# An expert stage with its overflow loop first, stores on another queue, aligned tiles, and a second norm moved into the gather

## The chip, the cores and the metric

The kernel runs on one core of one Trainium2 chip. The metric is the device time of one launch in microseconds, as the median of several runs. The engines are named as in the profile: PE is TensorE's matmul and PEld its weight load, DVE is VectorE, ACT is ScalarE, POOL is GpSimd, and SP is SyncE, which only issues transfers here. Each of SP, ACT and POOL can issue transfers on a queue of its own; a "q" behind an engine's name is its sequencer.

## The reference, cut to what matters

512 tokens of 1024 float32 values go through two transformer blocks. In the first, two mixers run side by side (a gated linear recurrence and a sparse attention), their outputs are merged and multiplied by `w_out`, and a layer norm follows. Then come a second norm with a scale and shift made from a conditioning vector, a router over 32 experts in 4 groups, two experts for each token, and a further layer norm. The second block is a causal attention and a gated feed-forward network, both with modulated RMS norms. The part that the change touches:

```python
mod = c_act @ ada_w[l] + ada_b[l]
sh1, sc1, g1, sh2, sc2, g2 = jnp.split(mod, 6, axis=-1)
...
y = (1 + g1[:, None]) * (merged @ w_out[l])
x = _layer_norm(ALPHA * x + y) * ln1_g[l] + ln1_b[l]
h = _layer_norm(x) * (1 + sc2[:, None]) + sh2[:, None]
y = (1 + g2[:, None]) * _hier_moe(h, router_grp_w[l], router_grp_b[l], ...)
x = _layer_norm(ALPHA * x + y) * ln2_g[l] + ln2_b[l]
...
return (jax.nn.silu(xb @ w1[e]) * (xb @ w3[e])) @ w2[e]      # one expert, 1024 -> 512 -> 1024
```

An expert has 6 MB of weights (three float32 matrices of 2 MB), so the 32 experts have 192 MB, and each of them is read once.

## The kernel before, in words

**Stages.** The first stage (up to about 735 us) computes the two mixers. Its large products go through `mm3` (lines 93 to 95): each operand is split into a high and a low part, and three matmuls (high by high, low by high, high by low) are added up in PSUM. Lines 75 and 77 split the weights as they arrive, ScalarE the high part and VectorE the low one. `finish_t1` (lines 1439 to 1533) does the product with `w_out`, the layer norm, the second norm and the router's logits; `router` ranks the tokens. `t2` (lines 487 to 769) is the expert stage. The rest, from about 1360 us, is the second block, with `mm3` again.

**The way from the output product to the first expert.** `finish_t1` multiplies in four blocks of 128 tokens by four column blocks of 256. After a block's last column, `layer_norm` (lines 166 to 185) makes the block's `x1`. Two things follow for each block: `logits` (lines 258 to 270) transposes x1 and multiplies it by the router's weights, whose scale has been folded in; `norm` (lines 272 to 277) makes the second norm, with two VectorE passes over 128x1024 (lines 181 and 183) that read their columns in a permuted order, a ScalarE copy to the high part `h2hi`, and a GpSimd subtraction for the low part. `SC2` and `SH2` are the scale and shift spread over all 128 partitions. A table `order` (lines 517 to 519) says which of these steps stand behind which product. The router then works on small tiles, mostly on VectorE, and gives each of the 1024 token copies a row: rows 64e to 64e + 63 belong to expert e, and rows from 2048 on hold what doesn't fit into 64.

**Tokens and experts.** `gather` (lines 500 to 529) builds a one-hot matrix from the rows and multiplies it by the high and low parts of the second norm (line 525, 64 matmuls for four experts), so that the tokens of four experts come out transposed, 64 columns each; lines 527 and 528 evict half of them by ScalarE and half by VectorE. `up` (line 541) multiplies the 64 tokens by w1 and w3, 16 matmuls each, and evicts (line 548). `act` transposes, applies the gate function (Silu, line 557, ScalarE) and multiplies (line 558, VectorE). `down` (line 570) multiplies by w2; line 575 applies g2 into a tile `y` (three buffers), and line 603 stores `y` to a DRAM array `yscr` with a DMA on GpSimd's queue. In program order expert e + 1's `up` stands ahead of expert e's `down`.

**Weights.** `Stream` (lines 410 to 456) holds a ring of 15 places of 1 MB for the expert weights: 4 tiles of its own, 3 `raw` tiles that the first stage's weights use too, 4 "late" tiles, which are there when the first stage has ended, and 4 pairs of `whi` and `wlo` parts. Each load (1 MB, line 454, or two halves, line 450) is issued by SP when its place has come free. The program issues 16 loads ahead of the experts (lines 468 to 484), the others as the ring goes round.

**The overflow loop.** `general` (lines 676 to 700) is a loop on the device over blocks of 64 tokens for experts with more than 64. With the timed inputs it makes no trip. It stands ahead of expert 18 (`CUT`, line 718); expert 18's `up` isn't issued ahead of expert 17's `down` then, and lines 737 to 742 issue the loads for the next places ahead of the loop. Line 679 is the loop's head, where all engines meet; line 720 is expert 18's `up` behind it.

**Behind the experts.** `late` (lines 648 to 674) reloads x1 and fetches the rows of `yscr`, and lines 753 to 766 add them up and apply the last layer norm.

**Order of the work.** The program is written in one order, and a planner with a cost model moves instructions of an engine within what the data allow; `issue_after` fixes a place. SBUF tiles come from pools, in which a tile stands wherever the one before it ended.

Of the kernel before, what the change touches and what calls it, by code (L numbers as in the profile page):

```python
# [9 lines left out]
F32 = mybir.dt.float32  # L10
F32R = mybir.dt.float32r
BF = mybir.dt.bfloat16
# [14 lines left out]
class G:  # L27
    pass

# [136 lines left out]
def layer_norm(g, pool, x, total, gain, bias, out, tag, accum=None, perm=False):  # L166
# [11 lines left out]
    if perm:  # L178
        x, gain, bias = (t.rearrange("q (p k) -> q k p", k=8) for t in (x, gain, bias))
        out = out.rearrange("q (k p) -> q k p", k=8)  # L180
    nc.vector.scalar_tensor_tensor(out, x, mv[:, 0:1], gain, op0=ALU.add, op1=ALU.mult)
    nc.vector.reciprocal(mv[:, 1:2], mv[:, 1:2])
    g.last_norm = nc.vector.scalar_tensor_tensor(out, out, mv[:, 1:2], bias, op0=ALU.mult, op1=ALU.add,
# [4 lines left out]
def iota(g, pool, shape, pattern, name, chan=0):  # L188
    t = pool.tile(shape, F32, name=name)
    g.nc.gpsimd.iota(t, pattern=pattern, base=0, channel_multiplier=chan, allow_small_or_imprecise_dtypes=True)  # L190
    return t


def route_state(g, pool):
# [10 lines left out]
    r.iot = iota(g, pool, [128, 256], [[1, 256]], "iot")  # L205
    r.pidx = iota(g, pool, [128, 1], [[0, 1]], "pidx", 1)
    r.II = pool.tile([128, 64], F32, name="II")
    nc.vector.tensor_tensor(r.II, g.ident[:, 0:64], g.ident[:, 64:128], op=ALU.add)


class Front:
# [3 lines left out]
    def __init__(self, g, pool, work, pp, ptags, x1d, sc2, sh2, mods, w_rg, w_re, b_rg, b_re):  # L215
        nc = g.nc
        self.g, self.pool, self.work, self.pp, self.ptags, self.x1d = g, pool, work, pp, ptags, x1d
        self.sc2, self.sh2, self.mv = sc2, sh2, {}
# [7 lines left out]
        cols = pool.tile([128, 2, 8], F32, name="cols")  # L226
# [45 lines left out]
    def norm(self, i, x, total, h2):  # L272

        g = self.g
        self.mv[i] = layer_norm(g, self.work, x, total, self.sc2, self.sh2, h2, "h2", perm=True)
        g.nc.scalar.activation(g.h2hi[:, i], h2, AF.Copy)
        g.nc.gpsimd.tensor_tensor(g.x_tile(F32R)[:, 0], h2, g.h2hi[:, i].bitcast(F32), op=ALU.subtract)
# [8 lines left out]
def router(g, f, pp, ptag, pbufs):  # L286

    nc, r, rp = g.nc, g.route, f.pool
# [38 lines left out]
    for i in range(4):  # L327
        for j in range(i):
            nc.tensor.matmul(rps[:, i], f.oneb, M[:, j], start=(j == 0), stop=False)
        nc.tensor.matmul(rps[:, i], f.tri, M[:, i], start=(i == 0), stop=True)  # L330
    gt = rp.tile([128, 32, 7], F32, name="gt")
# [18 lines left out]
    def rest(pool):  # L350
# [29 lines left out]
        nc.vector.scalar_tensor_tensor(r.row, ro, dx, r.row, op0=ALU.mult, op1=ALU.add)  # L380
        nc.vector.tensor_copy(r.rowi, r.row)
# [12 lines left out]
        nc.vector.tensor_scalar(r.obase, ok, 64.0, 1984.0, op0=ALU.mult, op1=ALU.add)  # L394
# [12 lines left out]
CUT = 18  # L407
# [55 lines left out]
def t2_early(g, pool, w1, w3, w2):  # L463

    st = g.stream = Stream(g, w1, w3, w2)
    st.add(pool, 4)
    st.add("raw", g.ws.nraw)
    for e in range(2):
        for j, h in UP:
            st.fetch(e, j, h)  # L470


def t2_ahead(g):

    st = g.stream
    for n in (4,):
        st.add(g.es2.enter_context(g.tc.tile_pool(name="t2late%d" % n, bufs=1, side="right", reuse_waits="tile")), n)
    st.add("parts", g.ws.nhi)
    for h in range(2):
        st.fetch(0, 2, h)  # L480
    for j, h in UP:
        st.fetch(2, j, h)
    for h in range(2):
        st.fetch(1, 2, h)


def t2(g, yscr, x1d, g2, ln2g_, ln2b_, ahead):
# [5 lines left out]
    with es:  # L493
        pp = es.enter_context(tc.tile_pool(name="t2p", bufs=1, space=PSUM))
        ee = es.enter_context(ExitStack())
        eg = ee.enter_context(tc.tile_pool(name="t2g", bufs=1, side="right"))

        h2 = [g.h2hi[:, i] for i in range(4)], [t[:, 0] for t in g.xt[F32R]]

        def gather(nblk, base, between=None):  # L500
# [9 lines left out]
            for i in range(4):  # L510
                o1 = eg.tile([128, 256], F32, name="o1", tag="o1", bufs=2)[:, :n]
# [7 lines left out]
            def step(s):  # L519
                ps = pp.tile([128, 8, 64], F32, name="gps", tag="gps", bufs=2)  # L520
                for k in range(8 // nblk):
                    c = 128 * (8 // nblk * s + k)
                    for i in range(4):
                        for q, part in enumerate(h2):
                            nc.tensor.matmul(ps[:, k * nblk:k * nblk + nblk], part[i][:, c:c + 128], oh[:, i],  # L525
                                             start=(i + q == 0), stop=(i + q == 4))
                nc.scalar.copy(xg[:, 8 * s:8 * s + 4], ps[:, 0:4])
                nc.vector.tensor_copy(xg[:, 8 * s + 4:8 * s + 8], ps[:, 4:8])
# [22 lines left out]
        def act(t):  # L551
# [4 lines left out]
            sg = ep.tile([128, 4, 64], F32, name="sg", tag="sg", bufs=4)  # L556
# [4 lines left out]
        def down(sgs, raw, stores):  # L561
# [10 lines left out]
            for yp, store in zip(yps, stores):  # L572
                if callable(store):
                    y = ep.tile([128, 512], F32, name="y", tag="y", bufs=3)
# [23 lines left out]
        def store_at(row):  # L598
# [4 lines left out]
            return lambda y: nc.gpsimd.dma_start(yscr[row:row + 64].rearrange("r (h n) -> h r n", h=2), y)  # L603
# [25 lines left out]
        def onehot_last():  # L629
# [4 lines left out]
            for i in range(4):  # L634
                o1 = eg.tile([128, 256], F32, name="o1", tag="o1", bufs=2)[:, 0:128]
# [40 lines left out]
        def general(lraw):  # L676

            nrun = nc.values_load(r.nov[0:1, 0:1], min_val=0, max_val=NOV - 1)
            with tc.For_i(0, nrun, 1):
# [4 lines left out]
                one = indirect_weights(r.eb[:, 0:1], lraw)  # L684
# [21 lines left out]
        ep = ee.enter_context(tc.tile_pool(name="t2e", bufs=1))  # L706
# [8 lines left out]

        s_ = behind(0, up(sources(0), raw(0)))
        for e in range(32):
            if e == CUT:
                general(lraw)
                s_ = behind(e, up(sources(e), raw(e)))  # L720

            ts = up(sources(e + 1), raw(e + 1)) if e + 1 not in (CUT, 32) else None
# [12 lines left out]
            elif e + 1 == CUT:  # L735

                n, lraw = st.n, alloc()
                todo = [x for k in range(6) for x in [(CUT + k,) + u for u in UP] +
                        [(CUT + k - 1, 2, h) for h in range(2 if k else 0)]]
                for x in todo:  # L740
                    if st.n - n < len(st.ring):
                        st.fetch(*x)
# [8 lines left out]
        with tc.tile_pool(name="t2f", bufs=1) as fp:  # L751
# [160 lines left out]
def t1(g, d):  # L912
# [3 lines left out]
    with top:  # L916
# [3 lines left out]
        hp = eh.enter_context(tc.tile_pool(name="t1h", bufs=1))  # L920
# [925 lines left out]
```

## Time and profile before

| | before |
|---|---|
| median of 3 runs | 2033.7 us (2032.71 to 2036.41) |
| profiled execution, its own time | 2033.85 us |
| its span | 2032.1 us |
| TensorE's mean granted clock | 0.969 |
| PE busy | 1900.2 us (94%) |
| DVE busy | 1013.8 us (50%) |
| ACT busy | 637.3 us (31%) |
| POOL busy | 111.9 us (6%) |
| moved by DMA | 394.75 MB, mean 194 GB/s |

How to read it: the span is the time from the first to the last recorded instruction, and the profiled execution's own time is a little longer. A share of busy time is a mean over stages that have different limits: the experts' weights are read in the slices from 820 to 1340 us, where the page shows about 405 GB/s, against 30 to 300 in the other slices. A busy share of the DMA is a mean over the core's 16 DMA engines. A matmul's duration overlaps its neighbours', so the step from one start to the next is what it costs in a run of them. The chain of waits names, for each stretch of the span, what the last work was waiting for; "issue" is time without a wait that the profile shows.

### The profile page before, as it was taken

To read this page: it belongs to the slowest core of one execution; us is meant where nothing else is said; L and a number is where in the kernel's file an instruction comes from. 1 tells how busy PE (TensorE), PEld (TensorE's weight loads), DVE (VectorE), ACT (ScalarE), POOL (GpSimd) and SP (SyncE) were. 2 spreads that over 40 slices of the span, in tenths; PEclk is the share of its full clock that TensorE was granted. 3 is DMA by queue.
4 is the path that set the end of the run, shared out by engine and by line. 5 is a ranking of instruction groups with operands and counts; after the bars stand their busy time and mean duration, and the time that the engine had idled before them with its cause. 6 is when DMAs were issued, how large, how long until landed. Compare 5 with 4: busy or idle time off the path is not lost.

```text
span 2032.1 us, 25738 instructions
## 1 busy us (share of the span) xinstructions
PE 1900.2 (94%) x10012; PEld 1364.3 (67%) x10012; DVE 1013.8 (50%) x1886; ACT 637.3 (31%) x1145; POOL 111.9 (6%) x187
## 2 busy tenths in 40 slices
PE   5999999999999998799996699789999999999998
PEld 4887888777678788445442244237777778888886
DVE  7776775577676548421110111047788853333222
ACT  4343243244532214110000011026656653223221
POOL 1100000010000012000000000031000000000000
PEclk7999999999999998898998799999999999999999
DMA  8525545733156575599999899982211122322321
GB/s 297 174 72 181 171 124 150 218 105 106 33 197 221 173 258 208 205 407 409 405 387 405 335 406 409 408 283 83 63 57 48 61 75 83 112 96 84 116 97 47
DMA packets 180435, 394.75 MB, mean 194 GB/s; under 512 B 24417, under 2 KB 104495, under 8 KB 162392
## 3 DMA queue, kind: packets, MB, share of 16 engines
q1 hardware_dynamic: 155511, 356.44, 48.5%
q0 software_dynamic: 24224, 34.55, 5.6%
q10 hardware_dynamic: 576, 2.10, 0.3%
q8 instruction: 80, 1.31, 0.3%
q14 instruction: 44, 0.35, 0.1%
HBM read 376.11 MB, written 16.83 MB: 193 GB/s over the span
## 4 chain that ended last, share of the span: by engine, by line
PE 78%; DMA 11%; DVE 7%; ACT 2%; issue 2%; SPq 0%; DVEq 0%; ACTq 0%; POOL 0%
PE pj L93 13%; PE pj L94 13%; PE pj L95 12%; PE A L541 8%; DMA xraw<-in_exp_w_dram 4%; PE yp L570 4%; PE gps L525 3%; PE pj L1712 3%; PE pj L1711 3%; PE pj L1713 3%; DMA whiraw<-in_exp_w_dram 3%; PE no L1380 2%; DMA raw<-in_exp_w_dram 2%; DMA wloraw<-in_exp_w_dram 2%; PE S L1362 2%
## 5 line engine op out<-in xcount | busy, mean ns | idle before, releaser
L93 PE MATMUL pj<-hhi,whi 128*128 128x512 f32 x880 | 355.2, 404 | 0.0
L95 PE MATMUL pj<-hhi,wlo 128*128 128x512 f32 x880 | 353.1, 401 | 2.0 <-DVE wlo L77 2.0
L94 PE MATMUL pj<-hlo,whi 128*128 128x512 f32 x880 | 353.3, 401 | 0.0
L77 DVE TENSOR_TENSOR wlo<-raw,whi 128x1024 fp32r<-128x1024 f32 x192 | 231.7, 1212 | 228.6 <-ACT whi L75 224.6
L75 ACT ACTIVATE whi<-raw 128x1024 fp32r<-128x1024 f32 x192 | 200.5, 1050 | 380.4 <-PE pj L94 159.8
L93 PEld LDWEIGHTS pj<-hhi,whi 128*128 128x128 f32 x880 | 166.4, 189 | 41.7 <-issue 6.8
L95 PEld LDWEIGHTS pj<-hhi,wlo 128*128 128x128 f32 x880 | 166.3, 189 | 38.3 <-issue 2.6
L94 PEld LDWEIGHTS pj<-hlo,whi 128*128 128x128 f32 x880 | 166.3, 189 | 35.6 <-issue 3.3
L541 PE MATMUL A<-xraw,xg 128*64 128x512 f32 x576 | 170.6, 597 | 10.5 <-DMA xraw<-in_exp_w_dram 10.5
L541 PEld LDWEIGHTS A<-xraw,xg 128*64 128x64 f32 x576 | 51.3, 137 | 95.4 <-issue 76.2
L548 ACT COPY ab<-A 128x512 f32<-128x512 f32 x33 | 19.3, 585 | 299.5 <-PE A L541 299.5
L575 DVE TENSOR_TENSOR y<-yp,g2t 128x512 f32<-128x512 f32 x31 | 21.4, 692 | 167.5 <-PE yp L570 167.5
L541 PE MATMUL A<-raw,xg 128*64 128x512 f32 x216 | 65.9, 611 | 35.0 <-DVE rb L506 35.0
L93 PE MATMUL pj<-whi,hhi 128*128 128x256 f32 x320 | 90.7, 283 | 0.0
L94 PE MATMUL pj<-wlo,hhi 128*128 128x256 f32 x320 | 89.9, 281 | 0.0
L95 PE MATMUL pj<-whi,hlo 128*128 128x256 f32 x320 | 89.9, 281 | 0.0
L525 PE MATMUL gps<-oh,h2hi 128*128 128x256 f32 (+1 forms) x288 | 77.7, 305 | 5.4 <-DVE oh L513 5.4
L525 PEld LDWEIGHTS gps<-oh,h2hi 128*128 128x128 f32 x288 | 58.0, 201 | 31.0 <-issue 30.0
L525 PE MATMUL gps<-oh,xt 128*128 128x256 f32 (+1 forms) x288 | 74.2, 293 | 0.0
L558 DVE TENSOR_TENSOR sg<-sg,gt 128x256 f32<-128x256 f32 x33 | 13.9, 420 | 120.3 <-ACT sg L557 120.1
L1712 PE MATMUL pj<-wlo,ahi 128*128 128x512 f32 x176 | 69.3, 394 | 0.0
L1711 PE MATMUL pj<-whi,ahi 128*128 128x512 f32 x176 | 69.0, 392 | 0.0
(508 smaller groups left out, 3501.6 us busy)
## 6 DMA issues: line engine op xcount, KB each, us to landing
xraw<-in_exp_w_dram SPq DMA_DIRECT2D x103, 1024.0 KB, 14.2
raw<-in_exp_w_dram SPq DMA_DIRECT2D x37, 1024.0 KB, 15.9
raw<-in_w_in_dram SPq DMA_DIRECT2D x34, 1024.0 KB, 6.0
wloraw<-in_exp_w_dram SPq DMA_DIRECT2D x52, 512.0 KB, 14.4
whiraw<-in_exp_w_dram SPq DMA_DIRECT2D x52, 512.0 KB, 14.3
araw<-in_ada_w_dram SPq DMA_DIRECT2D x48, 512.0 KB, 3.9
raw<-in_ffn_w_in_dram SPq DMA_DIRECT2D x22, 1024.0 KB, 5.1
raw<-in_ada_w_dram SPq DMA_DIRECT2D x19, 1024.0 KB, 5.8
```

Of the source, the lines that this page charges most:

```text
L75: self.last_hi = nc.scalar.activation(hi, rv, AF.Copy)
L77: self.last = nc.vector.tensor_tensor(lo, rv, hi.bitcast(F32), op=ALU.subtract)
L93: nc.tensor.matmul(ps, lh, rh, start=(i == 0), stop=False)
L94: nc.tensor.matmul(ps, lh, rl, start=False, stop=False)
L95: last = nc.tensor.matmul(ps, ll, rh, start=False, stop=(i == n - 1))
L525: nc.tensor.matmul(ps[:, k * nblk:k * nblk + nblk], part[i][:, c:c + 128], oh[:, i], start=(i + q == 0), stop=(i + q == 4))
L541: nc.tensor.matmul(ps[64 * j:64 * j + 64], xg[:, k, b], w[kk // 2][:, 512 * (kk % 2):512 * (kk % 2) + 512], start=(k == 0), stop=(k == 7))
L570: nc.tensor.matmul(yp[64 * nh:64 * nh + 64], sg[:, f], w[ff][:, 512 * nh:512 * nh + 512], start=(f == 0), stop=(f == 3))
L1362: nc.tensor.matmul(S[:, :n], qT[:, f, 128 * i:128 * i + 128], kT[kn][:, gg, 0:n], start=True, stop=True)
L1711: nc.tensor.matmul(ps[i], ah, hi, start=(k == 0), stop=False)
L1712: nc.tensor.matmul(ps[i], ah, lo, start=False, stop=False)
L1713: nc.tensor.matmul(ps[i], al, hi, start=False, stop=(k == nk - 1))
```

## The change

- **Loop first.** `general` runs between the first gather and expert 0's `up`. `CUT`, the loads issued ahead of it and the missing look-ahead at expert 18 go. One late tile, `lraw`, is set aside for the loop's weights. Overflow rows begin above row 2048 whenever the fixed blocks don't hold all.
- **16 places.** The ring has 5 tiles of its own for 4, and the loads are issued in a list `st.order` until all places are taken.
- **ScalarE stores.** Line 603's stores go by ScalarE's queue.
- **Aligned tiles.** Pools give tiles of 512 bytes or more a start that is a multiple of 64 bytes, and those of the large operands (`t1h`, `t1m`, `t3o`, `t3h`, `t3h2` and the weights' pool `w`) one of 256.
- **Second norm.** `norm` becomes `stats` (mean, square, root), `high` (ScalarE normalizes with permuted columns and copies the high part) and `low` (VectorE subtracts). Scale and shift are left out there; `cols2` holds them by the partition, and the evictions of `gather` apply them, ScalarE for even pieces and VectorE for odd ones. `SC2` and `SH2` go. The last block's `low` stands in the router, between the ranking matmuls and what follows.
- **Smaller things.** `iot` is bfloat16; `o1` has one buffer, `sg` three and `y` two; the router's tiles have a pool of their own.

The diff, cut to its core (in the pools' lines `tc.tile_pool(` becomes `sbuf(tc, ` throughout, and two stand for all):

```diff
+class Aligned:
...
+    def tile(self, shape, dtype, **kw):
+        size = 4 * math.prod(shape[1:])
+        n = self.least or (64 if size >= 512 else None)
+        return self.pool.tile(shape, dtype, align_bytes=n, **kw)
...
+    def stats(self, i, x, total):
...
+        nc.vector.tensor_scalar(mv[:, 0:1], total, -1.0 / 1024, None, op0=ALU.mult)
+        junk = self.work.tile([128, 1024], BF, name="ljunk", tag="ljunk", bufs=1)
+        nc.scalar.activation(junk, x, AF.Square, bias=mv[:, 0:1], accum_out=mv[:, 1:2])
+        nc.scalar.activation(mv[:, 1:2], mv[:, 1:2], AF.Sqrt, bias=g.eps5, scale=1.0 / 1024)
+        nc.vector.reciprocal(mv[:, 1:2], mv[:, 1:2])
+        nc.vector.tensor_tensor(mv[:, 2:3], mv[:, 0:1], mv[:, 1:2], op=ALU.mult)
+    def high(self, i, x, n):
...
+        nc.scalar.activation(n.rearrange("q (k p) -> q k p", k=8), x.rearrange("q (p k) -> q k p", k=8), AF.Identity,
+                             scale=mv[:, 1:2], bias=mv[:, 2:3])
+        nc.scalar.activation(g.nhi[:, i], n, AF.Copy)
+    def low(self, i, n):
...
-        self.mv[i] = layer_norm(g, self.work, x, total, self.sc2, self.sh2, h2, "h2", perm=True)
-        g.nc.scalar.activation(g.h2hi[:, i], h2, AF.Copy)
-        g.nc.gpsimd.tensor_tensor(g.x_tile(F32R)[:, 0], h2, g.h2hi[:, i].bitcast(F32), op=ALU.subtract)
+        g.nc.vector.tensor_tensor(g.x_tile(F32R)[:, 0], n, g.nhi[:, i].bitcast(F32), op=ALU.subtract)
...
-CUT = 18
+LATE = (4,)
...
-    st.add(pool, 4)
+    st.add(pool, 5)
     st.add("raw", g.ws.nraw)
...
+    st.order = [x for e in range(4) for x in [(e, j, h) for j, h in UP] + [(e - 1, 2, h) for h in range(2) if e]]
+    while st.n < len(st.ring):
+        st.fetch(*st.order.pop(0))
...
     st.add("parts", g.ws.nhi)
...
+    st.lraw = st.alloc()
+    while st.n < len(st.ring):
+        st.fetch(*st.order.pop(0))
...
-                nc.scalar.copy(xg[:, 8 * s:8 * s + 4], ps[:, 0:4])
-                nc.vector.tensor_copy(xg[:, 8 * s + 4:8 * s + 8], ps[:, 4:8])
+                for k in range(8 // nblk):
+                    dst, src = xg[:, 8 * s + k * nblk:8 * s + k * nblk + nblk], ps[:, k * nblk:k * nblk + nblk]
+                    sc, sh = (g.cols2[:, q, 8 // nblk * s + k:8 // nblk * s + k + 1] for q in range(2))
+                    if k % 2:
+                        nc.vector.tensor_scalar(dst, src, sc, sh, op0=ALU.mult, op1=ALU.add)
+                    else:
+                        nc.scalar.activation(dst, src, AF.Identity, scale=sc, bias=sh)
...
-            return lambda y: nc.gpsimd.dma_start(yscr[row:row + 64].rearrange("r (h n) -> h r n", h=2), y)
+            return lambda y: nc.scalar.dma_start(yscr[row:row + 64].rearrange("r (h n) -> h r n", h=2), y)
...
+        general()
         s_ = behind(0, up(sources(0), raw(0)))
         for e in range(32):
-            if e == CUT:
-                general(lraw)
-                s_ = behind(e, up(sources(e), raw(e)))
-
-            ts = up(sources(e + 1), raw(e + 1)) if e + 1 not in (CUT, 32) else None
+
+            ts = up(sources(e + 1), raw(e + 1)) if e < 31 else None
...
-        hp = eh.enter_context(tc.tile_pool(name="t1h", bufs=1))
+        hp = eh.enter_context(sbuf(tc, 256, name="t1h", bufs=1))
...
+    order = {(1, 3): ((logits, 0), (stats, 0), (high, 0), (stats, 1), (logits, 1), (low, 0), (high, 1)),
+             (2, 3): ((logits, 2), (low, 1)),
+             (3, 3): ((f.scale, 0), (f.scale, 1), (stats, 2), (f.scale, 2), (high, 2), (logits, 3), (stats, 3),
+                      (f.scale, 3), (high, 3), (low, 2))}
...
-    router(g, f, pp, "hU", 2)
+    router(g, f, pp, "hU", 2, lambda: low(3))
...
-    with tc.tile_pool(name="c", bufs=1) as cp, tc.tile_pool(name="w", bufs=1, side="right", reuse_waits="tile") as wp, \
+    with sbuf(tc, 32, name="c", bufs=1) as cp, sbuf(tc, 256, name="w", bufs=1, side="right", reuse_waits="tile") as wp, \
```

## Rows read from the trace of the kernel before

**Rows 1.** Busy by stretches: us, PE PEld DVE ACT POOL, PEclk, DMA, GB/s.

```profile
845.00:1085.00 240.00, 239.33 (x1212) 110.02 (x1210) 37.66 (x93) 24.34 (x54) 12.83 (x16) 0.98 1.02 401
...
1130.00:1145.00 15.00, 8.00 (x30) 2.54 (x32) 0.82 (x4) 0.00 (x0) 0.00 (x0) 0.66 0.53 178
```

**Rows 2.** Chain of waits, 700 to 1450, by time: start us, us.

```profile
826.41 9.35 PE gps L525 x64
...
835.76 7.02 PE A L541 x32
...
1087.34 17.07 DMA raw<-in_exp_w_dram
...
1121.52 14.27 DMA xraw<-in_exp_w_dram
...
1137.00 8.71 PE A L541 x32
...
1325.07 10.31 DMA xraw<-in_exp_w_dram
```

**Rows 3.** SyncE's waits: waiting line, releaser: us, times, longest us.

```profile
SPq L679 <- DMA xraw<-in_exp_w_dram: 13.0, 2, 10.6
```

**Rows 4.** The page's costliest groups: out<-in xcount | busy us, mean ns

```profile
L93 PE MATMUL pj<-hhi,whi 128*128 128x512 f32 x880 | 355.2, 404 | 0.0
...
L77 DVE TENSOR_TENSOR wlo<-raw,whi 128x1024 fp32r<-128x1024 f32 x192 | 231.7, 1212 | 228.6 <-ACT whi L75 224.6
...
L548 ACT COPY ab<-A 128x512 f32<-128x512 f32 x33 | 19.3, 585 | 299.5 <-PE A L541 299.5
...
L575 DVE TENSOR_TENSOR y<-yp,g2t 128x512 f32<-128x512 f32 x31 | 21.4, 692 | 167.5 <-PE yp L570 167.5
...
L558 DVE TENSOR_TENSOR sg<-sg,gt 128x256 f32<-128x256 f32 x33 | 13.9, 420 | 120.3 <-ACT sg L557 120.1
```

**Rows 5.** TensorE's timeline at 793, its last output product: start us, us.

```profile
793.23 0.28 PE L95 MATMUL pj<-whi,mlo 128*128 128x256 f32 x1
```

**Rows 6.** VectorE's groups by form, 780 to 814.5.

```profile
L183 DVE SCALAR_TENSOR_TENSOR xt<-xt,h2mv,SH 128x1024 f32<-128x1024 f32 x4 | 10.1, 2526 | 0.1
...
L181 DVE SCALAR_TENSOR_TENSOR xt<-ax,h2mv,SC 128x1024 f32<-128x1024 f32 x4 | 8.6, 2145 | 0.1
```

**Rows 7.** VectorE's timeline at 780 and 814: start us, us.

```profile
779.93 1.28 DVE L183 SCALAR_TENSOR_TENSOR ax<-ax,l1mv,l1b 128x1024 f32<-128x1024 f32 x1
...
814.02 0.17 DVE L294 TENSOR_REDUCE gm<-lg 128x4 f32<-128x16 f32 x1
...
814.84 2.28 DVE L303 TENSOR_TENSOR goh<-i,gmi 128x16 f32<-128x16 f32 x1
```

**Rows 8.** TensorE's groups by form, 796 to 812.

```profile
L270 PE MATMUL lps<-w_rm,h2T 128*128 128x36 f32 x32 | 7.3, 408 | 0.0
...
L267 PE MATMUL rt<-ident,ax 128*128 128x128 f32 x16 | 3.9, 421 | 5.7 <-DVE ax L183 5.7
```

**Rows 9.** DMA queues, 845 to 1085: packets, MB, share of 16 engines.

```profile
q1 hardware_dynamic: 15972, 91.96, 95.4%
...
q0 software_dynamic: 8282, 4.06, 5.9%
```

**Rows 10.** Line 603 on GpSimd: ns min/median/max, first and last start us.

```profile
L603 POOL DMA_DIRECT2D yscr<-y x30: 796/796/867, 856.8 to 1299.3; - x30
```

**Rows 11.** TensorE's timeline at 660 and 1800: start us, us.

```profile
659.92 0.39 PE L95 MATMUL pj<-hi,wlo 128*128 128x512 f32 x1
...
661.79 0.39 PE L94 MATMUL pj<-olo,whi 128*128 128x512 f32 x1
...
1799.84 0.39 PE L94 MATMUL pj<-hlo,whi 128*128 128x512 f32 x1
...
1801.88 0.39 PE L94 MATMUL pj<-hlo,whi 128*128 128x512 f32 x1
```

**Rows 12.** TensorE's groups by form, 0 to 735.

```profile
L93 PE MATMUL pj<-hhi,whi 128*128 128x512 f32 x432 | 177.7, 411 | 0.0
```

## What the change will do to the time

> **What bounds the kernel now.** Read the busy times by stretches first, then the chain of waits in order of time. The expert stage runs from the first expert matmul at 835.76 us to 1335.4, where the last weights land (1325.07 + 10.31) [rows 2]: 499.6 us. In 240 us of it the DMA engines are busy 1.02 of their time at 401 GB/s, and TensorE 239.3 us as well [rows 1]. Which of the two sets the end? TensorE comes to the end of its 18th expert in 1087.34 - 835.76 = 251.6 us [rows 2], 14.0 us an expert; 32 experts would need 447 us. The stage takes 53 us more, and the last pieces of the chain are loads. So TensorE runs ahead on the places filled before the start, uses them up, and the transfers set the end. A saving in this stage counts if it starts the stream of loads earlier, closes a hole in it, or makes its bytes cheaper. Before and behind the stage TensorE is busy nearly throughout, and its own steps set the time.
>
> **The loop moved.** The overflow loop at expert 18 made no trip, yet it cost. SyncE waited 13.0 us there for its own loads to land [rows 3]; the last landed at 1121.52 + 14.27 = 1135.8, and TensorE went on at 1137.0 [rows 2]. Until it went on no place came free and no load was issued, so the DMA moved 178 GB/s from 1130 to 1145 [rows 1]. Lost: 15 us x (401 - 178)/401 = 8.3 us of the stream that sets the end. With the loop first that hole goes: **-8.3**. TensorE's own pause, which was longer, cost nothing by itself, as loads streamed through most of it. In its new place the loop stands behind the first gather. Every engine must arrive there and pass the barrier: 1.2 us from the last landing to TensorE's next matmul at expert 18. Ahead of it the last gathered part has to be evicted (0.6, an eviction as L548's [rows 4]) and the count of trips read, and a cold start of TensorE may come behind it. I take 3.5 us: lower end 1.2, upper end 13, if loads are in flight at the barrier.
>
> **The way to the first gather.** From the last output product (793.23 [rows 5]) to the first gather matmul (826.41 [rows 2]) 33 us pass, in which TensorE mostly waits for VectorE. VectorE makes eight passes of the second norm in permuted order there, 10.1 + 8.6 us [rows 6], at 2.1 us or more, against 1.28 for a straight pass [rows 7]. They go. For them ScalarE makes one strided pass for each token block beside its copy, and VectorE one subtraction of 1.2 us (as L77's [rows 4]); GpSimd's four subtractions go too. Behind the last product there remain product added, mean, square, root and two straight passes, partly side by side: 3.7 us as an estimate, so the last x1 block is ready at 797.2. Its transposes and logits take half of 7.3 + 3.9 [rows 8], 5.6: 802.8. Scale 0.5, and I add 1 us for ScalarE, which has two squares, two strided passes and two copies in these 10 us. The strided pass on ScalarE isn't in the trace: between 1.2 (twice L548's half as long row, [rows 4]) and 2.1 (VectorE's permuted pass); I take 1.6, near the middle, and most of it is beside TensorE. The router starts at 804.3 instead of 814.02 [rows 7]: -9.7. In it one tiny instruction took 2.28 us, while GpSimd was subtracting, against 0.17 of its neighbours [rows 7]: -2.1. The last low part, +1.2, stands in the router's gap. First gather at 815.8, -10.6; less the loop's 3.5 the first expert starts 7 us earlier: **-7**, between +3 (loop at its upper end) and -11. What is late next is ScalarE's queue: if the planner puts the strided passes ahead of the logits' copies, 3 us of it are lost. The first loads are no limit, as their places come free with the last products, which don't move. One more place is worth at most one megabyte landed while the DMA idles, 2.6 us at 401 GB/s; the tile kept for the loop takes back as much unless it is filled right behind the loop: **-1.5**, between 0 and -2.6.
>
> **Stores by ScalarE.** In the 240 us GpSimd's queue took 5.9% of the DMA time for 4.06 MB, SyncE's 95.4% for 91.96 MB [rows 9]. At SyncE's price the 4.06 MB would cost 4.2%. The difference, 1.7% of 240 us, is 4.1 us for 16 stores, 0.26 each, 7.6 us for 30, all on the bound. Some of the surplus may be the store's shape (shorter rows than a load's): between 0 and -7.6, I take **-7**, near the row. On ScalarE the store waits for VectorE's multiply, and the next eviction is queued behind it; the up product of the next expert but one covers that. Two y buffers for three leave a store two experts' time, 28 us, to land.
> By the Trainium skill, page "Trainium Kernel Development and Optimization", section "Key Constraints", the DMAs of the SyncE, ScalarE and GpSimd queues run on the same 16 engines, and several issuers save issue time only. By that rule this term is 0 and the sum 2010; the two queues' unequal price by the byte in this trace speaks against it.
>
> **Aligned tiles.** One shape steps unequally in two places: 1.87 us for 8 steps at 660 (0.234 each), 2.04 for 9 at 1800 (0.227) [rows 11]. The two differ in the tiles that they read, not in shape. If a tile's place is the cause, the 432 x 3 steps of this shape in the first stage [rows 12] save 9.2 us; narrower ones may lose 1 to 2. Against it: nothing in the trace tells the tiles' places. Between +9 (the same spread the other way) and -18.5 (the same 7 ns on all 880 x 3 steps, [rows 4]). I take **-7**. Loads may get cheaper by the packet too; no row bears on it, 0. The gather's scale and shift ride on evictions that exist, and the single `o1`, the bfloat16 `iot` and three `sg` touch nothing on the bound: 0, hidden by the 36 us that TensorE has to spare in the stage (499.6 - 8.3 - 7 - 1.5 - 447).
>
> **Sum.** 8.3 + 7 + 1.5 + 7 + 7 = 30.8. The profiled execution took 2033.85 us (its span 2032.1 and 1.75 around it); the median of the three runs is 2033.7. 2033.85 - 30.8 = 2003.
>
> **Rivals.**
> A, the queue makes no difference: 2010. For it: equal bytes, equal engines. Against: the price by the byte [rows 9].
> B, alignment gives nothing: 2010. For it: no row names a place. Against: two constant steps of one shape [rows 11].
> C, alignment reaches the last stage or the loads too, 12 us more (18.5 for 7): 1991. For it: the change touches these tiles as well. Against: the last stage already has the smaller step.
> D, the loop finds loads in flight, as at expert 18, and waits 13 us for 3.5, with 3 us of the router's gain lost to ScalarE's queue: 2016. Against: all places come free around 793, 20 us ahead of the loop.
> E, slower: ScalarE's store stands ahead of the gate function that the next down product needs. TensorE then waits in each expert for an eviction, the multiply, the issue and the gate's product, 0.585 + 0.692 + 0.796 + 0.420 [rows 4, 10] = 2.5 us, 80 over 32 experts. The stage takes 447 + 80 = 527, 27 more than now; less 14 for start and alignment: 2047. It makes the kernel slower from 2.1 us an expert on ((499.6 + 14 - 447)/32). Against: a whole up product lies between.
> F, terms cancel (the steps lengthen by what the stage saves): within 4 us of before.
>
> **How the numbers follow.** Forecast 0.45, A 0.12, B 0.12, C 0.14, D 0.07, E 0.06, F 0.04. A measurement of this kernel can tell about 0.2%, 4 us, from no change. Faster: all but E and F, 0.90; same 0.04; slower 0.06. The range 1984 to 2021 holds the forecast with its ends, A, B, D and most of C; E, F and the tails are left out.
>
> **What would show it.** No hole in the stream of loads in mid-stage; the first expert matmul some 35 us behind the last product instead of 42; no permuted passes on VectorE; loads that take the whole DMA time but for some 4%; the first stage's steps at 0.227. It would be wrong if TensorE waited for ScalarE in each expert, if the barrier at the start took over 6 us, if the first stage's steps stayed, or if the last stage's moved.

## The result, and the profile after

The changed kernel takes 2152.16 us (median of 4 runs, 2149.89 to 2154.26) for 2033.2 before: a ratio of 1.0584, 95% interval 1.0563 to 1.0604. The forecast was 2003, range 1984 to 2021. The profiled execution has a span of 2152.3 us, 120.2 more than before. Where they are is seen by cutting the spans at four points of the timelines and the chain of waits [rows 2, 5]. The third kernel is the changed one with its stores back on GpSimd's queue (the first experiment):

| us | before | changed | stores by GpSimd |
|---|---|---|---|
| start to the last output product | 793.2 | 789.6 | 784.7 |
| to the first gather matmul | 33.2 | 27.1 | 27.1 |
| to the first expert matmul | 9.4 | 15.9 | 16.4 |
| to the landing of the last weights | 499.6 | 622.2 | 486.7 |
| to the end of the span | 696.7 | 697.5 | 693.6 |

The first row varies from trace to trace: the kernel of experiment 2, whose first stage is that of before, has 789.9, and those that share the changed kernel's first stage lie between 783.5 and 789.6. All of the loss is in the expert stage, 122.6 us. Busy time by stretches, for the stretch that [rows 1] show of before (us; PE, PEld, DVE, ACT and POOL busy; PEclk; DMA share; GB/s):

```profile
845.00:1085.00 240.00, 220.09 (x1060) 104.13 (x1056) 39.79 (x93) 22.73 (x48) 0.00 (x0) 0.93 0.77 305
```

The DMA engines, busy all the time before, stand at 0.77 and move 305 GB/s for 401. By the busy share they move as much as before (305 / 0.77 = 396 for 401 / 1.02 = 393): they are not slower, they are idle. What holds the loads back? SyncE's waits (engine and line that waited, releaser: us in total, times, longest) of the changed kernel:

```profile
SPq L487 <- DMA yscr<-y: 252.3, 17, 22.4
...
SPq L483 <- DMA yscr<-y: 117.3, 12, 21.2
...
SPq L715 <- DMA g2t<-md: 6.2, 1, 6.2
```

Lines 483 and 487 issue the expert weights. At 29 of them SyncE waited for the landing of a store of `y`, 369.6 us in all. A load writes a ring place and has nothing to do with `y`. The chain of waits shows what such a wait does (start us, us):

```profile
832.56 8.30 PE A L577 x32
...
889.35 3.46 PE yp L606 x16
892.83 0.70 DVE y L611
893.55 24.83 DMA yscr<-y
918.51 7.23 DMA xraw<-in_exp_w_dram
925.78 1.94 PE yp L606 x8
...
1439.72 15.06 DMA xraw<-in_exp_w_dram
```

The product of 889 gives `y`, its store is under way for 24.83 us, then a load is issued, lands in 7.2, and the next product can go on: transfers and products take turns. SyncE's timeline beside it (start us, us, form, count):

```profile
885.60 14.98 SPq L487 DMA_DIRECT2D xraw<-in_exp_w_dram  x5
900.83 1.61 SPq L487 DMA_DIRECT2D raw<-in_exp_w_dram  x3
918.51 2.41 SPq L487 DMA_DIRECT2D xraw<-in_exp_w_dram  x4
```

The loads that SyncE had issued by 902.5 (1.61 us behind 900.83) land while it waits to 918.5.

The queues in that stretch, to be read beside [rows 9] (packets, MB, share of 16 engines):

```profile
q1 hardware_dynamic: 11845, 69.51, 72.9%
q10 hardware_dynamic: 1791, 3.61, 3.9%
```

By the byte the ScalarE queue is cheaper than GpSimd's was, 1.08% for a megabyte (3.9 / 3.61) for 1.45 [rows 9], as the prediction had it. That saving is lost in the waits.

Two other steps of the change are as they were meant to be: the permuted passes are gone from VectorE [rows 6], the loop's hole is gone from mid-stage (SyncE's 13.0 us at its head [rows 3] have become 6.2 at the start, line 715 above). Whether the first stage got faster can't be told from one trace; experiment 8 tells it.

### The profile page after: what moved, and what is told of

Its sections match the earlier page's. It is cut to its first block, busy times and chain, and to the rows that moved or that the text cites. A ratio compares the mean times of both kernels' runs of the same rounds, so it can differ in the third digit from the quotient of the medians.

```text
span 2152.3 us, 25715 instructions
## 1 busy us (share of the span) xinstructions
PE 1958.8 (91%) x10012; PEld 1379.2 (64%) x10012; DVE 1004.4 (47%) x1891; ACT 653.3 (30%) x1153; POOL 75.0 (3%) x153
## 4 chain that ended last, share of the span: by engine, by line
PE 38%; DMA 19%; DVE 2%; ACT 1%; issue 1%; SPq 0%; DVEq 0%; ACTq 0%; POOLq 0%; POOL 0%
DMA yscr<-y 11%; DMA xraw<-in_exp_w_dram 6%; PE pj L112 5%; PE pj L111 5%; PE pj L113 5%; PE A L577 5%; PE yp L606 3%; PE pj L1744 3%; PE pj L1745 2%; PE pj L1746 2%; PE gps L556 2%; PE pv L1720 1%; DMA whiraw<-in_exp_w_dram 1%; PE tr L1707 1%; PE z L1686 1%
## 5 line engine op out<-in xcount | busy, mean ns | idle before, releaser
L577 PE MATMUL A<-xraw,xg 128*64 128x512 f32 x600 | 213.2, 660 | 55.7 <-DMA xraw<-in_exp_w_dram 55.5
L577 PEld LDWEIGHTS A<-xraw,xg 128*64 128x64 f32 x600 | 59.6, 150 | 175.0 <-issue 94.2
L606 PE MATMUL yp<-xraw,sg 128*64 128x512 f32 x304 | 83.6, 647 | 22.5 <-DMA xraw<-in_exp_w_dram 22.4
L556 PE MATMUL gps<-oh,nhi 128*128 128x256 f32 (+1 forms) x288 | 86.2, 327 | 7.3 <-DVE swx L401 4.7
L556 PEld LDWEIGHTS gps<-oh,nhi 128*128 128x128 f32 x288 | 62.9, 218 | 41.9 <-issue 33.9
L556 PE MATMUL gps<-oh,xt 128*128 128x256 f32 (+1 forms) x288 | 81.0, 310 | 4.8 <-issue 4.8
L577 PE MATMUL A<-raw,xg 128*64 128x512 f32 x192 | 70.7, 630 | 8.7 <-DMA raw<-in_exp_w_dram 8.7
L556 PEld LDWEIGHTS gps<-oh,xt 128*128 128x128 f32 x288 | 63.0, 219 | 9.1 <-issue 9.1
```

The source lines that it names most:

```text
L577: nc.tensor.matmul(ps[64 * j:64 * j + 64], xg[:, k, b], w[kk // 2][:, 512 * (kk % 2):512 * (kk % 2) + 512], start=(k == 0), stop=(k == 7))
L606: nc.tensor.matmul(yp[64 * nh:64 * nh + 64], sg[:, f], w[ff][:, 512 * nh:512 * nh + 512], start=(f == 0), stop=(f == 3))
```

## The experiments

**Theory T**: the loads wait for the stores because both are counted together. The compiled programs' own lists of instructions (no view of the profile) name the semaphores, the counters that an instruction waits for. Transfers by SyncE and ScalarE count their landing in one of eight, DMAHW0 to DMAHW7, taken in turn, and nearly every load of expert weights (233 of 240 in the changed kernel) waits for the count of its own, that is for the transfer eight before it. In the changed kernel ScalarE's stores take their turn among these eight; GpSimd's transfers have eight of their own (DMASW). Five loads of the changed kernel's SyncE, in order, the instructions between them left out (PE stands for the products that free the load's place). Number 2 is missing; it went to a store on ScalarE's queue:

```
L483 DMA wloraw<-in_exp_w_dram 128x1024 [waits DMAHW7_49,PE_49]
L487 DMA xraw<-in_exp_w_dram 128x2048 [waits DMAHW0_49,PE_49]
L487 DMA xraw<-in_exp_w_dram 128x2048 [waits DMAHW1_49,PE_49]
L487 DMA xraw<-in_exp_w_dram 128x2048 [waits DMAHW3_49,PE_49]
L487 DMA xraw<-in_exp_w_dram 128x2048 [waits DMAHW4_49,PE_49]
```

**1. Stores back on GpSimd.**

```diff
-            return lambda y: nc.scalar.dma_start(yscr[row:row + 64].rearrange("r (h n) -> h r n", h=2), y)
+            return lambda y: nc.gpsimd.dma_start(yscr[row:row + 64].rearrange("r (h n) -> h r n", h=2), y)
```

> The changed kernel with the 30 stores of y back on GpSimd's queue; nothing else differs. Theory T (a load on SyncE's queue waits until a ScalarE store issued a few transfers before it has landed, 369.6 us of such waits in the changed kernel): they vanish and with them the stage's 122.6 us, less the 8 to 10 us that the loop's hole and the 16th place give back; by spans 2032.1 - 3.2 (first expert earlier) + 0.8 (behind the stage) - 8 = 2022 us, and SyncE has no wait for y at its loads. Rival L (the loop at the start, the 16 places or the reserved tile upset the order of the loads): it stays at 2140 or above. Rival C (the stores' packets take the DMA engines' time, on whichever queue): it stays above 2100.

Measured: 2011.5 us, ratio to before 0.9913 (0.9898 to 0.9927). One line of the change costs 141 us; the rest of it gains 18.6. No wait for `y` is left at the loads, and the stretch stands as before:

```profile
845.00:1085.00 240.00, 237.73 (x1206) 110.50 (x1203) 46.77 (x109) 26.20 (x55) 12.84 (x16) 0.99 1.00 403
```

Rivals L and C fall. The time came out 10 us under T's figure, which was summed up from the changed kernel's start and tail.

**2. The kernel before, with ScalarE stores.** Line 603: `nc.gpsimd.dma_start` becomes `nc.scalar.dma_start`.

> The kernel before with only the 30 stores of y moved from GpSimd's queue to ScalarE's. Theory T: the waits of SyncE for the landing of y appear here too, 29 of them at about 12.7 us (369.6 / 29), the stage gets some 110 to 130 us longer: 2145 to 2165. Rival L (needs the loop first or the 16 places): 2034, within 0.5%. Rival Q (the queue is cheaper by the byte, as the prediction had it): 2027.

Measured: 2163.7 us, ratio 1.0657 (1.0637 to 1.0678). The edit alone makes the loss, without the loop, the places or the alignment. SyncE waited for `y` at 26 loads, for 29 forecast:

```profile
SPq L454 <- DMA yscr<-y: 221.1, 16, 22.8
...
SPq L450 <- DMA yscr<-y: 112.3, 10, 23.2
```

**3 and 4. Extra copies by ScalarE.** The kernel of experiment 1 with, for each store, a second transfer of P of the 128 partitions to an array that nobody reads, P = 64 and P = 16:

```diff
+                nc.scalar.dma_start(g.spare[row // 64, 0:P], y[0:P])
```

> The changed kernel with its stores on GpSimd's queue and, for each of the 30, an extra copy of the first 64 of y's 128 partitions by ScalarE's queue to an array that nobody reads. Theory T with the landing time as the cause: half the packets land in about half the time (some 10 to 12 us for 20 to 25), a load meets a store that has landed or nearly; the waits are far under half of the changed kernel's: 2020 to 2060. Rival N (each ScalarE transfer among the loads costs the same, whatever its size): 2140 or above. Rival C (the bytes of the stores on the DMA engines): 128 KB x 30 at 400 GB/s is 10 us: 2030.

> The changed kernel with its stores on GpSimd's queue and an extra copy of 16 of y's 128 partitions by ScalarE's queue to an array that nobody reads. Theory T: the copy lands in a few us, ahead of the load that would wait for it; no wait of SyncE for it over 2 us, 2011 to 2018. Rival N (each ScalarE transfer costs a fixed time, half of which the copy of 64 partitions showed as 41.6 us over 30): 2045 or above.

Measured, one run each: 2053.1 us for 64 partitions and 2043.8 for 16; 42 and 32 us over experiment 1. The copies landed in 6.2 and 4.6 us (medians of the pages). The first is within T's range, but its waits, 214.4 us, are 58% of the changed kernel's and not far under half. The second is far over T's 2011 to 2018 and close to N, whose fixed price is 32 us though, not the 141 of the changed kernel. SyncE's waits, first P = 64, then P = 16:

```profile
SPq L487 <- DMA spare<-y: 147.7, 17, 17.2
...
SPq L483 <- DMA spare<-y: 66.7, 12, 15.9
```

```profile
SPq L487 <- DMA spare<-y: 134.7, 17, 17.1
...
SPq L483 <- DMA spare<-y: 59.4, 10, 13.5
```

A copy of 16 partitions still makes waits of up to 17.1 us. The timeline of all engines (P = 16) tells why:

```profile
928.12 15.43 SPq L487 DMA_DIRECT2D raw<-in_exp_w_dram  x3
...
937.66 0.69 DVE L611 TENSOR_TENSOR y<-yp,g2t 128x512 f32<-128x512 f32 x1 [9.17 <-PE yp L606]
...
938.38 0.31 ACTq L641 DMA_DIRECT2D spare<-y  x1
...
943.79 2.62 SPq L487 DMA_DIRECT2D xraw<-in_exp_w_dram  x4
```

SyncE's three issues stretch from 928.12 to 943.55, with one wait of 13.0 us for a copy in them. ScalarE issued this copy only at 938.38, since VectorE made `y` at 937.66, and the loads went on 5 us behind it. So a load waits not only for a store to land, but for one that **is not issued yet**. SyncE runs as far ahead of the experts as there are places, in the order of the program; a store among the eight ends that. T needs two parts: this tie (32 us here, with the few us that a small copy takes to land), and the time that the changed kernel's stores take to land.

**5. SyncE's queue for the stores.** `nc.scalar.dma_start` becomes `nc.sync.dma_start`.

> The changed kernel with the stores of y on SyncE's own queue, the loads' queue. Theory T (a load waits until a store a few transfers before it has landed; SyncE's and ScalarE's transfers are counted together): the loads wait for the landing of y here too, and besides for VectorE's y: 2130 or above. Rival S (ScalarE's queue is the slow one, a store lands late only there): the store lands with the loads, 2010 to 2040.

Measured: 2229.6 us, one run. The forecast of T came true for its second reason: SyncE itself waits for VectorE's `y`, with all loads queued behind.

```profile
SPq L639 <- DVE y L611: 415.8, 30, 24.1
...
SPq L487 <- DMA yscr<-y: 16.5, 6, 3.4
...
SPq L483 <- DMA yscr<-y: 14.5, 7, 2.4
```

As the loads stand still by then, this says nothing of how long a store lands beside them; rival S is not tested by it; experiments 6 and 7 answer it.

**6 and 7. Why a store takes up to 26 us.** The changed kernel, ScalarE stores kept, with the half rows written one behind the other (6), and as two transfers to the same addresses as in the changed kernel (7):

```diff
-nc.scalar.dma_start(yscr[row:row + 64].rearrange("r (h n) -> h r n", h=2), y)
+nc.scalar.dma_start(yscr[row:row + 64].rearrange("r (h n) -> (r h) n", h=2), y)      # 6
+for h in range(2):                                                                  # 7
+    nc.scalar.dma_start(yscr[row:row + 64, 512 * h:512 * h + 512], y[64 * h:64 * h + 64])
```

> The changed kernel, its ScalarE stores kept, but each store writes its 128 half rows one behind the other in the array instead of in two interleaved sets (the later gather of rows then reads halves in the wrong order, so the output differs; no instruction is more or less). The copies of 16 and 64 partitions, written in that manner, cost 32 and 42 us over 30 experts, the changed kernel's stores 141. Theory T2 (two parts: SyncE can't run ahead of the experts' stores, some 32 us; and a store in two interleaved sets lands in 15 to 25 us, the rest): the flat store lands in under 8 us, 2040 to 2065. Rival T1 (256 KB on ScalarE's queue take 15 to 25 us in any layout): 2140 or above.

> The changed kernel, its ScalarE stores kept, but each y goes out as two stores of 64 partitions, one for each half of the row: the same bytes to the same places in the array, in transfers whose outermost dimension is 64 instead of 2. In the changed kernel the DMA's busy share falls to 0.14 while a store is the last to land, about two of the 16 engines. Theory W (a store with an outermost dimension of 2 runs on two engines, beside the loads' packets there, and lands late for that): all engines work on it, it lands in a few us, and only the price of tying SyncE's loads to the experts stays: 2035 to 2060, perhaps some us above the flat store's 2042.7 for the second transfer. Rival D (half rows at a stride of a row in DRAM are slow to write): nothing changes, 2140 or above.

Measured: 2042.7 us (ratio 1.006, 1.0042 to 1.0078) and 2041.5 (1.0063, 1.0043 to 1.0082). Both take 110 of the 141 us away, the second with the same bytes at the same places. The stores by the pages (KB each, median us from issue to landing), one line each from the kernel before, experiment 6 and experiment 7:

```profile
yscr<-y POOLq DMA_DIRECT2D x30, 256.0 KB, 18.4
...
yscr<-y ACTq DMA_DIRECT2D x30, 256.0 KB, 7.2
...
yscr<-y ACTq DMA_DIRECT2D x60, 128.0 KB, 6.7
```

ScalarE's queue lands these stores in 7 us, so rival S falls. And GpSimd's stores took 18.4 us in the kernel before, where SyncE has no wait for `y` at its loads: a late landing held the loads up only where they counted it. What makes the changed kernel's stores late is the shape of the transfer: with an outermost dimension of 2 it runs on two engines. ScalarE's queue over the whole span, in the changed kernel, experiment 6 and experiment 7 (packets, MB, share):

```profile
q10 hardware_dynamic: 4476, 9.96, 1.2%
...
q10 hardware_dynamic: 4896, 9.96, 1.3%
...
q10 hardware_dynamic: 5376, 9.97, 1.4%
```

The same bytes go out with 14 and 30 more packets for each of the 30 stores. The traces' packet records name them: beside 128 packets of 2048 bytes a store has packets of 4 bytes, 2 in the changed kernel, 16 in experiment 6, 32 in experiment 7. Read as one from each engine that takes part, that is 2 engines, 16, and twice 16. The busy time of the DMA in the changed kernel, when 14 engines have done their part of the loads and the store of 893.55 has not landed (last three columns as above: PEclk, DMA share, GB/s), and its queues there:

```profile
895.60:899.00 3.40, 3.40 (x18) 1.19 (x16) 0.79 (x2) 0.16 (x1) 0.00 (x0) 1.00 0.14 56
```

```profile
q1 hardware_dynamic: 23, 0.16, 10.9%
q10 hardware_dynamic: 19, 0.03, 2.7%
```

0.14 of 16 engines is 2.2. In the packet records of these 3.4 us stand two chains, in each of which a load's packet of 8192 bytes (0.309 us) and a store's of 2048 (0.084 us) take turns, so the loads' remainder (q1's 10.9%) is late on these two engines as well. At such a pair's 0.393 us a store's 64 packets for each engine take 25 us, an estimate from these durations, beside loads without a break. By the Trainium skill, page "DMA: Bandwidth & Descriptors", section "Why a DMA increments its semaphore by 16 and not by 1", a transfer issued by SyncE or ScalarE is divided over the largest number of engines, up to 16, that divides the slowest dimension of both its sides; with 128 in `y` and 2 in the array that is two engines, and the share of 0.14 agrees. In experiment 7 the share over the stretch is 0.92, and waits of up to 15.1 us stay, the tie with a landing of 6.7 us in it:

```profile
845.00:1085.00 240.00, 234.45 (x1181) 109.24 (x1178) 45.00 (x105) 26.20 (x55) 0.00 (x0) 0.99 0.92 365
```

```profile
SPq L483 <- DMA yscr<-y: 111.5, 19, 15.1
...
SPq L487 <- DMA yscr<-y: 65.4, 10, 14.0
```

The remaining experiments take the kernel of experiment 1 and size the other terms.

**8. Tiles without alignment.**

```diff
-        return self.pool.tile(shape, dtype, align_bytes=n, **kw)
+        return self.pool.tile(shape, dtype, **kw)
```

> As the changed kernel with its stores on GpSimd's queue, but the pools give every tile the place that it had without the alignment. Theory A (a tile's place sets the step of a 512-column matmul; first-stage steps 0.233 before, 0.227 after): the steps go back to 0.233, the last output product comes 3.7 us later than with aligned tiles (793.2 for 789.6), and the kernel is 3 to 9 us slower than the aligned one. Rival B (the steps come from something else in the change): steps of 0.227 stay, same time within 2 us.

Measured: 2021.5 us, ratio 0.9955 (0.9938 to 0.9972) for 0.9913: alignment gives 10.0 us by the medians, 8.5 by the ratios, at or above the upper end of the 3 to 9 forecast. TensorE's timeline, the first and the last of ten matmuls, nine steps apart, first unaligned, then aligned:

```profile
200.66 0.39 PE L113 MATMUL pj<-hhi,wlo 128*128 128x512 f32 x1
...
202.76 0.39 PE L113 MATMUL pj<-hhi,wlo 128*128 128x512 f32 x1
```

```profile
200.39 0.39 PE L111 MATMUL pj<-hhi,whi 128*128 128x512 f32 x1
...
202.43 0.39 PE L111 MATMUL pj<-hhi,whi 128*128 128x512 f32 x1
```

2.10 us for nine steps (0.233) and 2.04 (0.227). Theory A holds for the steps.

**9. No loop at all.** `general()` is left out of the program.

> The changed kernel with its stores on GpSimd's queue and the overflow loop left out altogether (tokens beyond an expert's 64 rows would not be computed; with these inputs there are none). From the first gather matmul to the first expert matmul the kernel before took 9.35 us, the one with the loop first 16.35. Theory: the 7 us are the loop's meeting point (5.1 us without a matmul, a late eviction, a slower restart), they go, the loads' stream moves up with them, and the time falls from 2011.5 to 2004 to 2007. Rival: transfers set the stage's end and places are free late anyway; within 2 us of 2011.

Measured: 2004.9 us, ratio 0.9870 (0.9852 to 0.9888). In its place at the start the loop costs 6.6 us by the medians, 8.7 by the ratios. From the first gather matmul to the first expert matmul it is 6.65 us (815.37 to 822.02) for 16.35.

**10. The loop back ahead of expert 18**, with 16 places, its own loads issued ahead and its tile taken there (`CUT`, the missing look-ahead and the list of loads as in the kernel before).

> The changed kernel with its stores on GpSimd's queue and the overflow loop back ahead of expert 18, with its loads issued ahead of it and the tile for it taken there. Leaving the loop out gave 2004.9 for 2011.5, so in its first place it costs 6.6 us. Theory P (the loop's hole in the stream of loads, 8.3 us by the trace of the kernel before, is the price at 18): 2004.9 + 8.3 = 2013, so the move is worth 0 to 3 us only. Rival (16 places and early loads carry the stream across the hole): 2005 to 2008, the move lost time. Rival (the hole grows with the faster rest): over 2018.

Measured: 2012.5 us, ratio 0.9911 (0.9894 to 0.9927). At 18 the loop costs 7.6 us (2012.5 - 2004.9; 8.3 by the ratios). P holds: the hole is worth about what the prediction said, and the move gives 1 us by the medians and nothing by the ratios, as the new place costs nearly the same.

**11. The load of g2 ahead of the first gather**, since SyncE waited 6.2 us for it at the loop's head.

> The changed kernel with its stores on GpSimd's queue and the load of g2 (two transfers on GpSimd's queue) ahead of the first gather instead of behind it, in the gather's pool. In the trace of the one with the load behind, SyncE waits 6.2 us at the loop's head for this load. Theory: that wait is most of the loop's price at the start; the pause falls by some 3 us, first expert 824 to 826 for 828.15, total 2007 to 2010. Rival: the meeting of the engines itself costs the 5 us: 2011 within 2 us.

Measured: 2012.8 us, ratio 0.9906 (0.9890 to 0.9922): no change. The rival holds. SyncE's wait for g2 at the loop's head is 1.6 us for 6.2, but one of 3.2 for VectorE stands beside it:

```profile
SPq L715 <- DVEq L714: 3.2, 1, 3.2
...
SPq L715 <- DMA g2t<-md: 1.6, 1, 1.6
```

**12. Logits ahead of the strided passes**, and the two last subtractions fixed behind the ranking.

```diff
-             (3, 3): ((f.scale, 0), (f.scale, 1), (stats, 2), (f.scale, 2), (high, 2), (logits, 3), (stats, 3),
-                      (f.scale, 3), (high, 3), (low, 2))}
+             (3, 3): ((logits, 3), (stats, 2), (stats, 3), (f.scale, 0), (f.scale, 1), (f.scale, 2),
+                      (f.scale, 3), (high, 2), (high, 3))}
...
+    with g.tc.issue_after(last.ins):      # last: the instruction that writes M
+        between()                         # low(2), low(3)
```

> The changed kernel with its stores on GpSimd's queue, and in the way to the first gather the last block's logits ahead of the strided ScalarE passes of blocks 2 and 3, and both last subtractions behind the router's ranking instead of inside its chain. First gather 27.1 us behind the last output product in the one without. Theory (the strided pass of 2.23 us stood ahead of the logits' copies, and VectorE waited 1.85 and subtracted 1.23 us in the router): 23 to 25 us, and 2007 to 2010 for 2011.5. Rival (the loads set the stage's end and don't start earlier): 2011 within 1.5 us.

Measured: 2009.4 us, ratio 0.9907 (0.9890 to 0.9923). The first gather comes 24.5 us behind the last product (786.38 to 810.92), as forecast, but the 2 us in the medians are within the intervals. Not settled. It is the fastest kernel here that keeps the loop, by its median.

**13. 15 places for 16.** `st.add(pool, 4)`.

> The changed kernel with its stores on GpSimd's queue and a ring of 15 places for 16 (4 tiles of its own for 5). Theory: one more place is worth at most a megabyte at the stage's start, 0 to 2.6 us: 2011.5 to 2014. Rival: with the loop first and one tile reserved, a place less leaves TensorE short of weights again and again: over 2018.

Measured: 2017.3 us, ratio 0.9937 (0.9921 to 0.9953). Neither: the place is worth 5.7 us by the medians (4.9 by the ratios), more than the megabyte that I counted and less than the rival said. The interval overlaps experiment 1's (0.9898 to 0.9927), so that it is worth more than 2.6 us is likely and not certain.

## Why the prediction was wrong, step by step

**Stores by ScalarE: the step that failed.** Forecast -7, measured +141. "Two y buffers for three leave a store two experts' time, 28 us, to land" asked only who waits for the buffer, and there it came out: VectorE waited once for a landed `y`, 1.0 us. It did not ask who else waits for a transfer to land. The answer stood in the trace of before, in lines of SyncE's waits that the prediction passed over:

```profile
SPq L450 <- DMA xraw<-in_exp_w_dram: 93.9, 47, 3.4
...
SPq L450 <- DMA raw<-in_exp_w_dram: 43.6, 21, 2.9
...
SPq L454 <- DMA xraw<-in_exp_w_dram: 30.8, 16, 2.5
```

A load that waits for the landing of a load to another place waits for a count, not for data. Before, such waits of a load were 3.4 us at most; that a transfer eight back on a full stream has nearly landed would explain it. A store in that row is tied to the expert that makes it (30 to 32 us in experiments 4, 6 and 7, 42 in experiment 3), and one on two engines lands late (110 us, experiments 6 and 7). No run gives ScalarE's stores semaphores of their own: the tie is shown by the programs' lists, by the waits that come and go with the queue and by the timeline of experiment 4, not by taking it away alone. The rule of the Trainium skill that the prediction weighed (page "Trainium Kernel Development and Optimization", section "Key Constraints"), that several issuers save issue time only, would have made the term 0. Neither that rule nor the forecast, which went by the DMA engines' time, has a term for waits, and the measured +141 came from waits.

Rival E had the sign and the edit, but not the mechanism or the size (2047). From 832 to 1455 us TensorE's matmuls waited for ScalarE three times, 2.0 us in all, and its weight loads 11 times, 9.5 us, never for the gate function; the store at 893.55 went 0.02 us behind VectorE's `y` (892.83 + 0.70). A, C, D and F don't hold either: the queue mattered, the last stage moved by 1.4 us only between experiments 8 and 1 (695.0 and 693.6), the loop cost 6.6 us for D's 13, though D's loss in ScalarE's queue came (2.6 us of it are undone in experiment 12, 27.1 - 24.5), and the terms did not cancel.

**The rest**, with the store's term left out, was forecast at -23.8 and measured at -18.6 (experiment 1). That it came so near is in part luck, as the start's miss and the place's gain offset each other. The terms below add up to some -20 to -23; the 2 to 5 us over -18.6 are not explained, and each term is known to some 4 us only.

- *Aligned tiles*: forecast -7, measured -8.5 to -10 (experiment 8). Right; rival B falls. That a tile's place sets the step is now shown, by the steps at one place in two kernels; [rows 11] alone left it open.
- *The hole in mid-stage*: forecast -8.3, measured -7.6 (experiment 10 against 9; -8.3 by the ratios). Right.
- *The loop in its new place*: forecast 3.5, measured 6.6 (experiment 9; 8.7 by the ratios), 7.0 by the trace (16.35 for 9.35). Mis-sized, within its bounds of 1.2 to 13; "over 6 us" at the barrier was one of the prediction's own signs of being wrong. The load of g2, for which SyncE waited, is not the reason (experiment 11).
- *The way to the first gather*: forecast -10.6, measured -6.1 (27.1 us for 33.2). Two terms were short, and both had been named. ScalarE's strided pass takes 2.23 us, for an upper end of 2.1; and it stood ahead of the logits' copies, the "3 us" of the prediction's late next. ScalarE's timeline in experiment 1's kernel:

```profile
791.52 2.23 ACT L297 ACTIVATE xt<-ax,h2mv 128x1024 f32<-128x1024 f32 x1 [1.00 <-DVE h2mv L292]
793.66 0.56 ACT L279 COPY h2T<-rt 128x512 f32<-128x512 f32 x1
```

- So the start, forecast -7, is +0.9 (27.1 + 16.35 for 33.2 + 9.35), and with it the first expert comes 43 us behind the last product, not 35.
- *One more place*: forecast -1.5, measured -5 to -6 (experiment 13), by its middle outside the bounds of 0 and -2.6, though the intervals do not settle that. Why it is worth more than the megabyte that fills it was not tried.
- *A reading that was off*: 1087.34 is not the end of the 18th expert, but the point at which TensorE begins its `up`; VectorE makes that expert's `y` at 1102.04. By then it had done 19 blocks, 18 experts and one block of overflow rows, in 266.3 us, 14.0 each; all 33 (L548 in [rows 4]) need 463 us for 447, and TensorE's 36 us to spare were about 20. That the transfers set the stage's end still stands (499.6), and no term that failed hung on it.

## What to carry to other kernels

When a transfer moves to another queue, ask who counts its landing, not only who uses its buffer: here a wait for the landing of an unrelated transfer meant that the two share a semaphore, and a transfer that depends on computation then held back those counted with it. How late the store lands is a second question: on GpSimd's queue 18 us made no load wait. Look at the outermost dimension of a store before its bytes: 256 KB with an outermost 2 took up to 26 us to land, and as two transfers of 64 rows cost 110 us less over 30 of them. The loop that makes no trip cost 7 to 8 us by the medians in mid-stage and 6 to 7 at the start; moving it was worth 1 us at most.

## What the runs showed of the hardware that was not expected

A transfer of 128 packets on two engines delays the loads as well, because their packets on these engines queue with it: the DMA stood at a share of 0.14 and 56 GB/s for 3.4 us with 23 packets of the loads and 19 of a store moved in that time, in turns of 0.309 and 0.084 us. And the step of a 512-column matmul depends on where the tiles stand: 0.233 us without alignment, 0.227 with it, at a granted clock of 1.00 (2.4 GHz).
